# Two more chunk pairs per feed-forward stage by seven products, the weight pools taken in another order, and the bias broadcasts cut in eight

## The chip, the core and the metric

The kernel runs on one core of one Trainium2 chip. A core has five engines that work side by side, each through its own list of instructions in order: TensorE (PE) multiplies matrices into PSUM, VectorE (DVE) and ScalarE (ACT) do elementwise work, GpSimd (POOL) does small elementwise work and issues some transfers, SyncE (SP) issues most transfers. They wait for each other by semaphores. The metric is the device time of one execution, in microseconds (us); the time of a kernel is the median of its runs.

## What is computed

Two layers, each of three stages on a sequence of 512 tokens with 1024 features, all in 32-bit floats. Every stage ends in a residual sum and a layer norm.

```python
D_MODEL, SEQ, DEPTH, D_FF = 1024, 512, 2, 2816

def _swiglu(x, w1, w2):
    gt, up = jnp.split(x @ w1, 2, axis=-1)
    return (jax.nn.silu(gt) * up) @ w2

for l in range(DEPTH):
    x = _layer_norm(DN_ALPHA * x + 0.5 * _swiglu(x, ffn1_w1[l], ffn1_w2[l]), ln1_g[l], ln1_b[l])
    mix = _token_mix(x, w_in[l], ..., rel_bias, w_br_a[l], w_br_b[l], w_br_c[l], w_gate[l], b_gate[l], w_out[l])
    x = _layer_norm(DN_ALPHA * x + mix, ln2_g[l], ln2_b[l])
    x = _layer_norm(DN_ALPHA * x + 0.5 * _swiglu(x, ffn2_w1[l], ffn2_w2[l]), ln3_g[l], ln3_b[l])
```

`_swiglu` is the feed-forward stage (FFN). It occurs four times, twice in each layer, and is what the change touches. `_token_mix` holds three kinds of attention; one of them adds a bias that depends on the distance of two tokens and is made from `rel_bias`.

## The kernel before

**Precision by three products.** A matrix product in 32-bit precision is made of three products in a faster format: each operand is split into a rounded part and the rest (`hi` and `lo` for weights, `xh` and `xl` for the activations), and hi·xh + hi·xl + lo·xh is summed in PSUM. A weight chunk therefore goes through three steps: a transfer into one of three `raw` buffers (L153), a rounding copy into `hi` on ScalarE (L146), and `lo = raw - hi` on VectorE (L147).

**The first half of an FFN.** `w1` has 2 x 2816 columns, in chunks of 128. A *pair* f (0 to 21) is the chunk of the gate and the chunk of the up part that belong together; it makes one tile `ha` or `hb` of the hidden layer, 128 features by 512 tokens. Pairs 0 and 1 are done by `staged`, in token halves, while the transposes of the last tokens still arrive. Pairs 2 to 21 run in the loop of `ffn` (L392 on), in one of two ways:

- A *plain* pair (f in `PLAIN`, L275): two projections, each 8 chunks of features x 3 products with 512 columns, so 48 matmuls (L167 to L169). Then `evac` (L332) computes silu times up: one step on ScalarE (L334), two on VectorE (L335, L336).
- A *seven-product* pair (`strassen`, L349, its weights from `seven`, L280): the pair is written as a product of 2x2 blocks (gate and up by the two halves of the features; tokens in two halves), and seven block products replace eight. Each is 4 x 3 matmuls with 256 columns, so 84 matmuls in all (L357). They need sums of weights (`ws`, L293 to L296), split like weights (L298, L299) into the units `u1` and `u2`; half of the up chunk split alone (`dh`, `dl`, L300, L301); and four sums of tokens, split into `th` and `tl`. The token sums are made once in each FFN, by `token_sums` (L305 to L320), in VectorE's order behind pair 2's call. The products come in a fixed order: the gate's unit `ug`, `u1` with the first token sum, `u1` with the second, `u2` with the third, `ud` with the fourth, then `ug` and `u2` with the tokens themselves. VectorE then puts the results together (L368 to L376).

**Where split weights lie.** A *unit* is one `hi` and one `lo` tile. `unit` (L130) hands them out in turn from a list `seq` of pools, position `more.n % len(seq)`: three from `wt`, two from `more.pool` where that is open (it is, in every FFN), two from `nx.w1` while the loop of pairs runs. `nx.w1` is the pool `w1p`, which is opened when the pairs begin and lies where `xa` was, the tokens in their untransposed form (and, in the first FFN, where the tables of `init` were). Its tiles can be written only when those have been read: `xa` is first sent to `x_sp` in HBM by four transfers from POOL's queue (L381). `th`, `tl`, `dh`, `dl`, `ws`, `sn` and `v` lie in `w1p` too. The counter `more.n` runs on from one stage to the next, so an FFN begins its pairs at whatever place of the list the counter has reached: in the first FFN that is the first of the two `w1p` units.

**The start of the kernel.** The first FFN also runs `tables` between the pairs of `staged` and pair 2: on TensorE some small products (L1281, L1287) and transposes (L1292, L1294), on VectorE the tables `ctab`, `vm`, `peT`, `bgate`. Two rows of bias values go to `bsml` in HBM (L1299), and from there two transfers spread them to `bvec`, 8 heads x 128 rows x 384 values each, 1.57 MB (L395). The attention of the first mix stage reads `bvec` from 381.9 us of the span on (L496).

**The second half of an FFN** (`rows_ln`) multiplies the hidden layer with `w2`, 22 row chunks, 24 matmuls of 512 columns each (L180 to L182), and ends in the layer norm. Two hidden tiles are split early, into a unit of `wt`, when pair 21 is reached.

**Order.** TensorE's and POOL's instructions run in the order of the program text. Those of VectorE, ScalarE and SyncE are ordered when the kernel is built, by a planner that estimates when each becomes ready. Each engine then keeps its order: an instruction that waits holds back all behind it.

Of the kernel before, what the change touches and what calls it, by code (L numbers as in the profile page):

```python
# [9 lines left out]
F32 = mybir.dt.float32  # L10
# [8 lines left out]
P = 128  # L19
S, D, F = 512, 1024, 2816  # L20
KD, KF, NB = D // P, F // P, S // P
H, DH, NSLOT = 8, 64, 32
# [4 lines left out]
TLEN = 3 * P  # L27
# [37 lines left out]
def body(tc, a, out, depth=DEPTH):  # L65
    nc = tc.nc
    PE, POOL = mybir.EngineType.PE, mybir.EngineType.Pool

    def pool(name, bufs=1, side=None, **kw):
        return tc.alloc_tile_pool(name=name, bufs=bufs, side=side, **kw)  # L70

    const = pool("const")
    xtp = pool("xtp")
    wt = pool("wt")
# [6 lines left out]
    def ps(tag=None, name="ps", shape=(P, 512)):  # L81
        if tag is None:
            tag = PS_ALL[ring[0] % 8]
            ring[0] += 1
        return psp.tile(list(shape), F32, name=name, tag=tag, bufs=PS_TAGS[tag])
# [16 lines left out]
    bgate = const.tile([P, depth, 3, KD], F32, name="bgate")  # L102
    peT = const.tile([P, depth, 2, 32], F32, name="peT")
    stats = [const.tile([P, 8], F32, name=f"st{i}") for i in range(NB)]
    const.tile([P, 48], F32, name="pad")

    xh = xtp.tile([P, KD, S], F32R, name="xh")
    xl = xtp.tile([P, KD, S], F32R, name="xl")
# [1 line left out]
    bsml = dram.tile([2, H, TLEN], F32, name="bsml")  # L110
    bvec = dram.tile([2, H, P, TLEN], F32, name="bvec")
# [6 lines left out]
    more = K()  # L118
# [9 lines left out]
    nx = K()  # L128
    nx.pool = nx.w1 = None

    def unit():

        if nx.pool:
            pl, nb = nx.pool, 4
        else:
            seq = [(wt, 3)] * 3 + [(more.pool, 2)] * 2 * bool(more.pool) + [(nx.w1, 2)] * 2 * bool(nx.w1)
            more.n += 1
            pl, nb = seq[more.n % len(seq)]
        return [pl.tile([P, KD, P], F32R, name=n, tag=n, bufs=nb) for n in ("hi", "lo")]
# [123 lines left out]
    def staged(wts, pend):  # L263

        pts = [ps(name="pj") for _ in wts]
        for i, (o, w) in enumerate(zip(pts, wts)):
            proj(o, w, halves[0])
            if i in pend:
                pend[i]()
        for o, w in zip(pts, wts):  # L270
            proj(o, w, halves[1])
        return pts

    NTAIL = 4
    PLAIN = (0, 1, 2, 3, 4, 5, 14)  # L275

    def ffn_first(w1):
        return [wcols(w1, c) for c in (0, F, P, F + P)]
# [1 line left out]
    def seven(w1, f):  # L280

        v = w1.rearrange("(k p) f -> p k f", p=P)
        rg, ru = wraw(), wraw()
        nc.sync.dma_start(rg, v[:, :, f * P:(f + 1) * P])
        nc.sync.dma_start(ru, v[:, :, F + f * P:F + (f + 1) * P])
        ug, u1, u2 = wsplit(rg), unit(), unit()
        ud = [nx.w1.tile([P, 4, P], F32R, name=n, tag=n) for n in ("dh", "dl")]
        h1, h2 = slice(0, 4), slice(4, 8)  # L290
        x1, x2 = [nx.w1.tile([P, KD, P], F32, name="ws", tag="ws", bufs=2) for _ in range(2)]
        tt = nc.vector.tensor_tensor
        tt(x1[:, h1], ru[:, h1], ru[:, h2], op=OP.add)  # L293
        tt(x1[:, h2], x1[:, h1], rg[:, h1], op=OP.subtract)  # L294
        tt(x2[:, h1], rg[:, h1], ru[:, h1], op=OP.subtract)
        tt(x2[:, h2], rg[:, h2], x1[:, h2], op=OP.subtract)  # L296
        for (hi, lo), x in ((u1, x1), (u2, x2)):
            nc.scalar.activation(hi, x, AF.Copy)  # L298
            tt(lo, x, hi.bitcast(F32), op=OP.subtract)  # L299
        nc.scalar.activation(ud[0], ru[:, h2], AF.Copy)  # L300
        tt(ud[1], ru[:, h2], ud[0].bitcast(F32), op=OP.subtract)  # L301
        return ug, u1, u2, ud
# [20 lines left out]
    def ffn(l, w1, w2, which, xap, xa, wts, pend, done_prev, last, nxt):  # L323


        st = K()
        NA = KF - NTAIL

        def hpart(f):
            return (st.ha, st.hb)[f >= NA][:, f - NA * (f >= NA)]  # L330

        def evac(f, pg, pu):  # L332
            t = st.lnp.tile([P, S], F32, name="t", tag="t", bufs=3)
            nc.scalar.activation(t, pg, AF.Tanh, scale=0.5)  # L334
            nc.vector.scalar_tensor_tensor(t, t, 1.0, pg, op0=OP.add, op1=OP.mult)  # L335
            nc.vector.tensor_tensor(hpart(f), t, pu, op=OP.mult)  # L336

        hs = {}

        def h_parts(k, t):  # L340
            nc.scalar.activation(t[:, 0], hpart(k), AF.Copy)
            nc.vector.tensor_tensor(t[:, 1], hpart(k), t[:, 0].bitcast(F32), op=OP.subtract)
            hs[k] = t

        H1, H2 = slice(0, 256), slice(256, 512)

        def strassen(f, ws):
            (ug, u1, u2, ud), (t1, t2, t3, t4) = ws, st.t
            ga, pa, pb = ps(name="pg"), ps(name="pu"), ps(name="pv")  # L349
            p_, r_, s_ = [(xh[:, k:k + 4, c], xl[:, k:k + 4, c]) for k, c in ((0, H1), (4, H1), (4, H2))]  # L350

            def prod(o, w, k0, x, first=True):
                for k in range(4):
                    hi, lo = w[0][:, k0 + k], w[1][:, k0 + k]
                    vh, vl = x[0][:, k], x[1][:, k]
                    for i, (wx, vx) in enumerate(((hi, vh), (hi, vl), (lo, vh))):
                        nc.tensor.matmul(o, wx, vx, start=first and k == 0 and i == 0, stop=k == 3 and i == 2,  # L357
                                         skip_group_check=True)

            tt = nc.vector.tensor_tensor  # L360
            prod(ga[:, H1], ug, 0, p_)
            prod(ga[:, H2], u1, 0, t1, False)
            sn = st.w1p.tile([P, S], F32, name="sn", tag="sn", bufs=2)
            nc.scalar.activation(sn, ga, AF.Copy)
            prod(pa[:, H1], u1, 4, t2)
            prod(pa[:, H2], u2, 0, t3, False)
            v = st.w1p.tile([P, S], F32, name="v", tag="v", bufs=2)
            tt(v[:, H1], pa[:, H1], sn[:, H1], op=OP.add)  # L368
            tt(v[:, H2], pa[:, H2], v[:, H1], op=OP.add)
            prod(pb[:, H1], ud, 0, t4)  # L370
            u = hpart(f)
            tt(u[:, H1], pb[:, H1], v[:, H2], op=OP.add)
            tt(u[:, H2], sn[:, H2], v[:, H2], op=OP.add)
            prod(ga[:, H1], ug, 4, r_, False)
            prod(ga[:, H2], u2, 4, s_, False)
            tt(ga[:, H2], ga[:, H2], v[:, H1], op=OP.add)  # L376
            evac(f, ga, u)

        pts = staged(wts, pend)
        for tb in range(NB):  # L380
            nc.gpsimd.dma_start(x_sp[tb * P:(tb + 1) * P, :], xa[tb])  # L381
        done_prev()
        xap.release()
        fb = pool("fb", reuse_waits="tile")
        st.lnp = pool("lnp", reuse_waits="tile")
        fa = pool("fa", reuse_waits="tile")
        st.hb = fb.tile([P, NTAIL, S], F32, name="hb")
        st.ha = fa.tile([P, NA, S], F32, name="ha")
        st.w1p = nx.w1 = pool("w1p", side="right", reuse_waits="tile")
        evac(0, pts[0], pts[1])  # L390
        evac(1, pts[2], pts[3])
        for f in range(2, KF):  # L392
            if after and f in (10, 14):
                i = after.pop()
                nc.gpsimd.dma_start(bvec[i], bsml[i, :, None, :].to_broadcast([H, P, TLEN]))  # L395
            if f == KF - 1:
                for k, n in enumerate(("hi", "lo")):
                    h_parts(k, wt.tile([P, KD, P], F32R, name=n, tag=n, bufs=3)
                            .rearrange("p (a b) c -> p a (b c)", a=2))
            if f not in PLAIN:  # L400
                strassen(f, seven(w1, f))
                continue
            wg, wu = wcols(w1, f * P), wcols(w1, F + f * P)
            pg, pu = ps(name="pg"), ps(name="pu")
            proj(pg, wg)
            proj(pu, wu)
            evac(f, pg, pu)
            if f == 2:
                token_sums(st)
        nx.w1 = None  # L410
        st.w1p.tile([P, 88], F32, name="pad")
        st.w1p.release()
        xap, xa = alloc_xa()
        for tb in range(NB):
            nc.gpsimd.dma_start(xa[tb], x_sp[tb * P:(tb + 1) * P, :])
        hsp = pool("hsp", side="right", reuse_waits="tile")
        ln = LN(hsp, which, l, xa, 0.25, last)

        def wload(k):
            if k not in hs:  # L420
                h_parts(k, hsp.tile([P, 2, S], F32R, name="hs", tag="hs", bufs=6))
            return wrows(w2, k)

        wts, pend = rows_ln(KF, wload, lambda k: hs[k][:, 0], lambda k: hs[k][:, 1], ln, NA, fa.release, nxt)

        def done():
            nx_close()
            hsp.release()
            st.lnp.release()
            fb.release()  # L430

        return wts, pend, done, xap, xa
# [812 lines left out]
            pre.append(wcols(first_w, 0, 2))  # L1245
            pre.append(wcols(first_w, F, 2))

    after = [0, 1]
    init = pool("init", side="right")

    def tables_load():
# [110 lines left out]
```

## Time and profile before

| | us |
|---|---|
| median of 3 runs | 2520.06 (2519.49 to 2521.06) |
| profiled execution, its own time | 2518.52 |
| its span on the core | 2516.8 |
| TensorE busy in the span | 2484.7 |
| VectorE busy | 1617.8 |
| ScalarE busy | 1077.9 |
| GpSimd busy | 213.1 |

The profile is of one execution. A row of a timeline has the start in us from the span's start, the time in us, the engine, the line, the operation, output<-inputs, the shape and a count of merged instructions; in brackets stand the engine's idle time before it and what ended that. A matmul's time there is longer than the distance to the next, since matmuls overlap in the array; what a matmul costs is the distance between two starts. The row of a group has a count, the busy time and the mean of one in ns, then the idle time before them. In the rows of slices each digit is the busy share of a fortieth of the span, in tenths; PEclk is TensorE's granted clock in tenths of full speed.

### The profile page before, as it was taken

How to read it: one execution, taken by the hardware profiler on the slowest of the kernel's cores; microseconds unless marked ns; L12 is line 12 of the kernel's file. 1: busy time of each engine (PE TensorE's matmuls, PEld its weight loads, DVE VectorE, ACT ScalarE, POOL GpSimd, SP SyncE). 2: the span in 40 equal slices, each digit the busy share in tenths (PEclk: the TensorE clock that was granted, in tenths of full speed). 3: DMA queues.
4: the chain of work that ended last, by engine and by line, in shares of the span. 5: the costliest groups of instructions: out<-in, count | busy, mean ns of one | idle time of the engine just before them, and what ended most of it. 6: DMA issues, size and time to landing. Idle time of an engine off the chain costs nothing.

```text
span 2516.8 us, 39571 instructions
## 1 busy us (share of the span) xinstructions
PE 2484.7 (99%) x15259; PEld 2173.9 (86%) x15259; DVE 1617.8 (64%) x3309; ACT 1077.9 (43%) x2107; POOL 213.1 (8%) x424
## 2 busy tenths in 40 slices
PE   7999999999999999999999999999999999999998
PEld 7999888788888888998889998877888888899987
DVE  5788455577753468884477883556776534788834
ACT  3344333476642233443343442345766322344432
POOL 2000000133300000000000000001332000000000
PEclk8999999999999999999999999999999999999999
DMA  7333434633143342334332353435321434323431
GB/s 235 91 105 110 152 102 124 180 86 85 47 138 97 122 126 83 111 109 151 117 109 76 105 163 102 140 109 155 89 77 43 146 101 139 109 77 109 140 127 59
DMA packets 378476, 286.11 MB, mean 114 GB/s; under 512 B 17928, under 2 KB 349848, under 8 KB 378288
## 3 DMA queue, kind: packets, MB, share of 16 engines
q1 hardware_dynamic: 370496, 258.68, 35.1%
q0 software_dynamic: 7792, 24.91, 2.7%
q8 instruction: 120, 1.97, 0.3%
q14 instruction: 68, 0.56, 0.1%
HBM read 256.22 MB, written 17.88 MB: 109 GB/s over the span
## 4 chain that ended last, share of the span: by engine, by line
PE 47%; DVE 1%; DMA 1%; ACT 1%; issue 0%; POOL 0%; DVEq 0%; POOLq 0%; ACTq 0%; SPq 0%
PE pg L357 7%; PE pu L357 3%; PE acc L181 3%; PE acc L180 3%; PE acc L182 3%; PE pj L167 3%; PE pj L168 3%; PE pj L169 3%; PE pv L357 2%; PE gate L167 1%; PE gate L168 1%; PE gate L169 1%; PE brp L169 1%; PE brp L168 1%; PE brp L167 1%; PE sN L881 1%
## 5 line engine op out<-in xcount | busy, mean ns | idle before, releaser
L147 DVE TENSOR_TENSOR lo<-raw,hi 128x1024 fp32r<-128x1024 f32 (+2 forms) x354 | 416.0, 1182 | 524.9 <-ACT hi L146 514.4
L146 ACT ACTIVATE hi<-raw 128x1024 fp32r<-128x1024 f32 (+2 forms) x354 | 359.8, 1025 | 717.9 <-PE acc L181 225.4
L167 PE MATMUL pj<-xh,hi 128*128 128x512 f32 (+1 forms) x720 | 266.7, 370 | 0.1
L168 PE MATMUL pj<-xl,hi 128*128 128x512 f32 (+1 forms) x720 | 254.7, 354 | 2.3 <-DVE xl L227 2.3
L169 PE MATMUL pj<-xh,lo 128*128 128x512 f32 (+1 forms) x720 | 254.5, 353 | 0.0
L180 PE MATMUL acc<-hi,hs 128*128 128x512 f32 x640 | 249.5, 390 | 0.0
L182 PE MATMUL acc<-lo,hs 128*128 128x512 f32 x640 | 249.1, 389 | 0.0
L181 PE MATMUL acc<-hi,hs 128*128 128x512 f32 x640 | 249.0, 389 | 0.0
L357 PE MATMUL pg<-xh,lo 128*128 128x256 f32 x720 | 203.8, 283 | 0.0
L357 PE MATMUL pg<-xl,hi 128*128 128x256 f32 x720 | 203.8, 283 | 0.0
L357 PE MATMUL pg<-xh,hi 128*128 128x256 f32 x720 | 203.7, 283 | 0.0
L298 ACT ACTIVATE hi<-ws 128x1024 fp32r<-128x1024 f32 x120 | 126.0, 1059 | 161.1 <-DVE ws L294 52.2
L299 DVE TENSOR_TENSOR lo<-ws,hi 128x1024 fp32r<-128x1024 f32 x120 | 145.8, 1219 | 36.1 <-ACT hi L298 36.0
L169 PEld LDWEIGHTS pj<-xh,lo 128*128 128x128 f32 x720 | 136.1, 189 | 19.7
L167 PEld LDWEIGHTS pj<-xh,hi 128*128 128x128 f32 x720 | 136.5, 190 | 15.3 <-issue 3.1
L168 PEld LDWEIGHTS pj<-xl,hi 128*128 128x128 f32 x720 | 136.7, 190 | 14.8 <-DVE xl L227 3.2
L181 PEld LDWEIGHTS acc<-hi,hs 128*128 128x128 f32 x640 | 120.2, 188 | 24.9
L182 PEld LDWEIGHTS acc<-lo,hs 128*128 128x128 f32 x640 | 120.1, 188 | 24.9
L180 PEld LDWEIGHTS acc<-hi,hs 128*128 128x128 f32 x640 | 120.2, 188 | 24.6
L357 PEld LDWEIGHTS pg<-xl,hi 128*128 128x128 f32 x720 | 138.2, 192 | 0.3
L357 PEld LDWEIGHTS pg<-xh,hi 128*128 128x128 f32 x720 | 138.2, 192 | 0.3
L357 PEld LDWEIGHTS pg<-xh,lo 128*128 128x128 f32 x720 | 138.2, 192 | 0.0
(323 smaller groups left out, 6016.5 us busy)
## 6 DMA issues: line engine op xcount, KB each, us to landing
raw<-in_ffn_w_dram SPq DMA_DIRECT2D x264, 512.0 KB, 3.8
raw<-in_w_in_dram SPq DMA_DIRECT2D x56, 512.0 KB, 4.0
raw<-in_w_gate_dram SPq DMA_DIRECT2D x48, 512.0 KB, 3.9
x_sp<-xa POOLq DMA_DIRECT2D x24, 512.0 KB, 5.1
ks<-hl SPq DMA_DIRECT2D x96, 128.0 KB, 2.4
xa<-x_sp POOLq DMA_DIRECT2D x16, 512.0 KB, 4.5
raw<-in_w_out_dram SPq DMA_DIRECT2D x16, 512.0 KB, 3.4
tab<-bvec SPq DMA_DIRECT2D x16, 256.0 KB, 4.1
```

Of the source, the lines that this page charges most:

```text
L146: nc.scalar.activation(hi[:, c], raw[:, c], AF.Copy)
L147: nc.vector.tensor_tensor(lo[:, c], raw[:, c], hi[:, c].bitcast(F32), op=OP.subtract)
L167: nc.tensor.matmul(o, hi[:, k], vh, start=first, stop=False)
L168: nc.tensor.matmul(o, hi[:, k], vl, start=False, stop=False)
L169: nc.tensor.matmul(o, lo[:, k], vh, start=False, stop=last)
L180: nc.tensor.matmul(o, sh(k)[:, t], hi[:, c], start=k == 0, stop=False)
L181: nc.tensor.matmul(o, sl(k)[:, t], hi[:, c], start=False, stop=False)
L182: nc.tensor.matmul(o, sh(k)[:, t], lo[:, c], start=False, stop=k == nk - 1)
L298: nc.scalar.activation(hi, x, AF.Copy)
L299: tt(lo, x, hi.bitcast(F32), op=OP.subtract)
L357: nc.tensor.matmul(o, wx, vx, start=first and k == 0 and i == 0, stop=k == 3 and i == 2, skip_group_check=True)
L881: nc.tensor.matmul(o[:, 0:nb].rearrange("p k b j -> p (k b j)"), q, kx[:, 2 * b0:2 * (b0 + nb)].rearrange("p a b -> p (a b)"), start=i == ...
```

## The change

Three edits, in four places of the text, and a tile that gets a name:

- `PLAIN` shrinks from seven pairs to five: pairs 4, 5 and 14 go over to seven products, pair 12 becomes plain. Of the 22 pairs, 17 go by seven products instead of 15, in each of the four FFNs. The first seven-product pair is now pair 4 instead of pair 6, and the runs between plain pairs are 8 and 9 long instead of 8 and 7.
- `unit` takes the pools, while `w1p` is open, in the order `wt`, `more`, `more`, `w1p`, `w1p`, `wt`, `wt`, and the counter is set to 4 when `w1p` opens, so that every FFN begins at the sixth place: three units of `wt`, two of `more`, two of `w1p`, and round again. The number of units is the same.
- The broadcasts to `bvec` are issued in eight transfers of two heads each, at pairs 6 to 13 instead of two transfers at pairs 10 and 14; ahead of each, POOL copies one column of the hidden tile of three pairs before into `pace`, a column of a tile that was there as padding, and so waits until that tile exists.

```diff
@@
-    const.tile([P, 48], F32, name="pad")
+    pace = const.tile([P, 48], F32, name="pace")[:, 0:1]
@@ def unit():
         if nx.pool:
             pl, nb = nx.pool, 4
         else:
-            seq = [(wt, 3)] * 3 + [(more.pool, 2)] * 2 * bool(more.pool) + [(nx.w1, 2)] * 2 * bool(nx.w1)
+            seq = [(wt, 3)] * 3 + [(more.pool, 2)] * 2 * bool(more.pool)
+            if nx.w1:
+                seq = seq[2:] + [(nx.w1, 2)] * 2 + seq[:2]
             more.n += 1
             pl, nb = seq[more.n % len(seq)]
@@
-    PLAIN = (0, 1, 2, 3, 4, 5, 14)
+    PLAIN = (0, 1, 2, 3, 12)
@@ def ffn(...):
         st.w1p = nx.w1 = pool("w1p", side="right", reuse_waits="tile")
+        more.n = 4
         evac(0, pts[0], pts[1])
         evac(1, pts[2], pts[3])
         for f in range(2, KF):
-            if after and f in (10, 14):
-                i = after.pop()
-                nc.gpsimd.dma_start(bvec[i], bsml[i, :, None, :].to_broadcast([H, P, TLEN]))
+            if after and f >= 6:
+                i, h = after.pop(0)
+                nc.gpsimd.tensor_copy(pace, hpart(f - 3)[:, 0:1])
+                nc.gpsimd.dma_start(bvec[i, h:h + 2], bsml[i, h:h + 2, None, :].to_broadcast([2, P, TLEN]))
@@
-    after = [0, 1]
+    after = [(i, h) for i in range(2) for h in range(0, H, 2)]
```

## The prediction

> **What bounds the kernel now.** I read the page's first lines, then TensorE's timeline where pairs begin, then the places where it waits.
>
> ```profile
> span 2516.8 us, 39571 instructions
> PE 2484.7 (99%) x15259; PEld 2173.9 (86%) x15259; DVE 1617.8 (64%) x3309; ACT 1077.9 (43%) x2107; POOL 213.1 (8%) x424
> ...
> PEclk8999999999999999999999999999999999999999
> ```
>
> TensorE is busy 99% of the span, and its clock is full but for the first fortieth. So the time can fall in two ways: fewer or shorter matmuls, or the removal of one of its few waits. The starts of pairs show what a pair costs.
>
> ```profile
> 60.94 0.39 PE L167 MATMUL pg<-xh,hi 128*128 128x512 f32 x1
> ...
> 71.82 0.39 PE L167 MATMUL pg<-xh,hi 128*128 128x512 f32 x1
> ...
> 103.65 0.28 PE L357 MATMUL pg<-xh,hi 128*128 128x256 f32 x1
> ...
> 113.73 0.28 PE L357 MATMUL pg<-xh,hi 128*128 128x256 f32 x1
> ```
>
> These are the starts of the plain pairs 3 and 4 and of the seven-product pairs 7 and 8 of the first FFN. A plain pair takes 71.82 - 60.94 = 10.88 us (48 matmuls, 0.2267 each), a seven-product pair 113.73 - 103.65 = 10.08 (84 matmuls, 0.120 each).
>
> The large wait is ahead of pair 2 of the first FFN:
>
> ```profile
> 34.17 3.21 PE L1281 MATMUL ct<-init,init 128*128 128x32 f32 x28
> ...
> 38.79 0.30 PE L1294 MATMUL peT<-ident,init 64*128 64x64 f32 x2
> 46.66 0.79 PE L167 MATMUL pg<-xh,hi 128*128 128x512 f32 x1 [7.58 <-ACT hi L146]
> ...
> 49.13 0.63 PE L168 MATMUL pg<-xl,hi 128*128 128x512 f32 x1
> 49.56 0.63 PE L169 MATMUL pg<-xh,lo 128*128 128x512 f32 x1
> ```
>
> TensorE stands still for 7.58 us until ScalarE has rounded pair 2's weights. After that two matmuls lie 0.43 apart instead of 0.227: the clock has halved. Pair 2 takes 60.94 - 46.66 = 14.28 us, 3.40 more than its neighbour.
>
> **Part 1: two more pairs by seven products.** In each FFN three plain pairs of 10.88 become seven-product pairs and one goes the other way: 2 x 0.80 = 1.60 us, over four FFNs 6.40. This stands only if VectorE keeps up, since a seven-product pair gives it much more to do.
>
> ```profile
> 1044.20:1064.30 20.10, 20.10 (x170) 20.10 (x169) 17.35 (x27) 10.73 (x14) 0.00 (x0) 1.00 0.55 157
> 1064.30:1075.20 10.90, 10.90 (x50) 9.05 (x49) 10.87 (x18) 3.21 (x4) 0.00 (x0) 1.00 0.33 98
> ```
> ```profile
> 1045.06 1.22 DVE L299 TENSOR_TENSOR lo<-ws,hi 128x1024 fp32r<-128x1024 f32 x1
> ```
> ```profile
> 1054.25 0.28 PE L357 MATMUL pg<-xh,hi 128*128 128x256 f32 x1
> ```
>
> The first two rows are windows of the second FFN (columns: length, then busy time of PE, weight loads, DVE, ACT, POOL, then clock, DMA share, GB/s). VectorE has 17.35 us in two seven-product pairs, 8.7 of 10.08 each. Pair 13, last of a run of eight, starts at 1054.25; its `u1`, used 1.44 us into it (one product of 12 x 0.120 down), was split by 1046.28: 9.4 us ahead. Since VectorE's 8.7 is below 10.08, a run of nine keeps most of that lead; if it lost a whole 1 us with the ninth, nothing would wait.
>
> The tight place is new: the first seven-product pair is pair 4, only two plain pairs (21.8 us) behind the start of pair 2, and VectorE must have made the token sums by then. Rows of the second FFN before:
>
> ```profile
> 940.15 0.40 PE L167 MATMUL pg<-xh,hi 128*128 128x512 f32 x1
> ```
> ```profile
> 940.95 4.62 DVE L314 TENSOR_TENSOR ha<-xh,xl 128x1024 f32<-128x1024 f32 x4
> 945.50 2.35 DVE L147 TENSOR_TENSOR lo<-raw,hi 128x1024 fp32r<-128x1024 f32 x2
> 947.76 1.22 DVE L317 TENSOR_TENSOR hb<-ha 128x1024 f32<-128x1024 f32 x1
> ...
> 952.90 1.22 DVE L320 TENSOR_TENSOR tl<-hb,th 128x1024 fp32r<-128x1024 f32 x1
> 954.04 0.68 DVE L293 TENSOR_TENSOR ws<-raw 128x512 f32<-128x512 f32 x1
> 954.64 0.68 DVE L295 TENSOR_TENSOR ws<-raw 128x512 f32<-128x512 f32 x1
> ```
>
> Pair 2 starts at 940.15; VectorE's token sums cannot start before 940.95, since their place in `ha` held the weights of `staged`. From there on, by the distance between starts (1.14 for 1024 columns, 0.60 for 512), the changed build lists this ahead of the last split token sum: the four sums 4.55; four differences and four splits 8 x 1.14 = 9.1; four weight sums and one of pair 5, 5 x 0.60 = 3.0; `dl` 0.60; splits of `u1`, `u2` and of pair 5's `ug` 3 x 1.14 = 3.4; three evacuation steps 1.8. In all 22.5: done at 963.4. The product that needs it is the fifth, 48 x 0.12 = 5.76 into pair 4, which starts at 940.15 + 21.8 = 961.9: at 967.7. That leaves 4.3 us; `u2`, done at 961.7 and needed at 966.3, has 4.6. The splits of pairs 2 and 3 and of pair 4's `ug` stand ahead of 940 in the build, so they are not in the sum. I take a wait of 0 here; the bounds are 0 and 4 us in each of three FFNs (a slip of twice the margin).
>
> The Trainium skill's page "TensorE: Matmul & The Clock Gate" (section "Wait — 56ns, not 53.3ns?") puts a warm matmul at N / 2.4 GHz plus 2.5 ns, so 215.8 ns for 512 and 109.2 for 256 columns; as an estimate by it a swap would save 48 x 0.2158 - 84 x 0.1092 = 1.19 us and part 1 would be 9.5. The starts above give 0.227 and 0.120, and the measurement decides.
>
> **Part 2: the pools turned.** Why pair 2 waits:
>
> ```profile
> 24.44 1.07 POOL L381 DMA_DIRECT2D x_sp<-xa  x2 [0.22 <-issue]
> 25.54 0.22 POOL L1297 TENSOR_SCALAR sinks<-sinks 128x16 f32<-128x16 f32 x1
> 39.07 0.57 POOL L1299 DMA_DIRECT2D bsml<-init  x1 [13.31 <-DVE init L1288]
> 41.50 0.52 POOL L1299 DMA_DIRECT2D bsml<-init  x1 [1.86 <-DVE init L1288]
> 44.98 2.22 POOL L395 DMA_DIRECT2D bvec<-bsml  x2 [2.96 <-DMA bsml<-init]
> ```
> ```profile
> 38.44 1.06 ACT L146 ACTIVATE hi<-raw 128x1024 fp32r<-128x1024 f32 x1 [4.71 <-DVE ctab L1283]
> 44.61 2.95 ACT L146 ACTIVATE hi<-raw 128x1024 fp32r<-128x1024 f32 x3 [5.12 <-DMA raw<-in_ffn_w_dram]
> ```
>
> Pair 2 gets the two `w1p` units, which lie over `xa` and `init`. `init` is read last by the second transfer to `bsml`, issued at 41.50 and landed just before 44.98, where POOL stops waiting for it. ScalarE's order has these two roundings as the second and third of the group at 44.61, behind a weight that landed then; two of three raw buffers hold pair 2's weights all that time, so the others go through one.
>
> After the change pair 2 takes two units of `wt`, one unused, one free when TensorE leaves the first weight of `staged`. That is three weights ahead of the end of `staged`, of 24 x 0.120 = 2.9 us each, which is where `ct` begins: 34.17 - 3 x 2.9 = 25.5. With 1.06 on ScalarE and 1.22 on VectorE it is ready by 28, and pair 2 can start when the transposes end, 38.79 + 0.30 = 39.09. Gain: 46.66 - 39.09 = 7.57, and 3.40 for the clock, which then stays full.
>
> What is late next? Pair 3 has `wt` and `more`, free at 28.4 and 31.3 by the same count. Pair 4 (due at 39.09 + 21.8 = 60.9) has `more`, then both `w1p` units, and `dh`, `th`, `tl` lie over `xa` and `init` too; all are open when `bsml` has landed, by 45. VectorE then has four splits of token sums, weight sums, `dl`, three splits and an evacuation, about 12 us: ready near 54, 8 us before `u1` is due. So the cover is there; without it this gain would turn into a wait at pair 4.
>
> The Trainium skill (same page, "Part 1: The HAM clock gate") has the clock halve after an idle window of about 3.4 us and return after about 3.4 us of work; by that, as an estimate, the restart would cost half of 3.4, 1.7 us, not the 3.40 of the row, and the sum be 16.5. The trace stayed slow for longer, and it decides.
>
> In the other three FFNs pair 2 waits for nothing (pair 3 follows 10.9 us behind), so the turn gains nothing there. The last pair of the first FFN gains:
>
> ```profile
> 245.59 0.28 PE L357 MATMUL pg<-xh,hi 128*128 128x256 f32 x1
> ...
> 248.05 0.38 PE L357 MATMUL pg<-th,lo 128*128 128x256 f32 x1 [0.61 <-DVE lo L299]
> ...
> 256.54 0.40 PE L180 MATMUL acc<-hi 128*128 128x512 f32 x1
> ```
>
> Pair 21 takes 10.95, 0.87 too long: its units were all of `wt` and `more`, with one `wt` unit lent to the hidden tiles, so one waited for pair 20. With the count begun anew it gets two `w1p` units and a `wt` unit last used by pair 19, as in the three FFNs that have no such wait. Gain 0.87.
>
> **Part 3: the broadcasts.** The same bytes in eight pieces. POOL has no other work from 47.2 us on for the 189.3 of its next wait, so the copies, 0.22 each by its smallest row above, hold up nothing.
>
> ```profile
> POOL xa L415 <- PE pg L357: 189.3, 1, 189.3
> ```
> ```profile
> raw<-in_ffn_w_dram SPq DMA_DIRECT2D x264, 512.0 KB, 3.8
> ...
> bvec<-bsml POOLq DMA_DIRECT2D x2, 1536.0 KB, 13.9
> ```
>
> A quarter of a broadcast's 13.9 us, 3.5, bounds from above what a piece can add to a weight transfer's 3.8; below, 0. It meets a pair every 10 us whose split weights are some 9 us ahead, and the next transfers wait for TensorE's release anyway, so delays don't add up: 0. Without that lead it would be up to 8 x 3.5 = 28 us. The burst that now ties up the transfers from 45 to 61 us is gone, which only adds cover.
>
> **Part 4: the rest.** Outside the FFNs the build gives every engine the same order as before; `pace` is the former padding. Nothing.
>
> **The sum.** 6.40 + 7.57 + 3.40 + 0.87 = 18.24 us. The span of 2516.8 becomes 2498.6, the profiled execution's 2518.52 becomes 2500.3. The median of the runs, 2520.06, lies 1.54 above that execution, so I expect 2520.06 - 18.24 = 2501.8, and with a rest for small waits at the new changes between kinds of pairs 2502.
>
> **Rivals.**
>
> *A, short waits at pair 4 of the later FFNs.* For: 22.5 us of VectorE's work in 26.8, in fixed order between ScalarE's steps. Against: 4.3 us of margin, counted at measured distances. Up to 4 us in each of three FFNs: 2503 to 2514.
>
> *B, the start still waits.* If the wait at 46.66 were due to the weights' arrival and not to where they are put, the 10.97 us stay: 2520.06 - 6.40 - 0.87 = 2512.8. For: ScalarE's row at 44.61 names a transfer. Against: the group's first weight waited for that, and TensorE was let go by a rounding whose place was the pool over `x`.
>
> *C, slower: the token sums become the bound.* In the three later FFNs the last token sum would come so late that TensorE stands still as long as it now does at the start, and its clock halves: 3 x (7.57 + 3.40) = 32.9 lost against 18.2 gained, 2534.7. It decides from a wait of 6.1 us in each (18.2 / 3), so from sums 10.4 us later than I count. For: VectorE has worked 85% of this stretch before (37.16 of 43.50 us):
>
> ```profile
> 940.20:983.70 43.50, 43.50 (x194) 35.99 (x194) 37.16 (x42) 14.08 (x16) 0.00 (x0) 1.00 0.25 73
> ```
>
> Against: with pairs 4 and 5 still plain, that stretch also held the preparation of pairs 6 to 8; what pair 4 needs is the first 22.5 us of it.
>
> *D, no gain per pair.* If VectorE's waits for ScalarE and transfers made a seven-product pair in a run of nine as long as a plain one, and B held too, the time would stay: 2519. Against: every seven-product pair of the profile but the last of the first FFN takes 10.08.
>
> **How the numbers follow.** My forecast has 0.70, A 0.12, B 0.08, C 0.06, D 0.04. The likeliest time is 2502. Its own range reaches down to 2499.5 (the runs before spread 1.6 us, and a wait I don't count may go) and, with most of A, up to 2511; B, C and D are left out, 0.18. A measurement of this kernel tells a change from none at 0.2%, 5.0 us. Faster by more: the forecast, A and B, 0.90; within: D, 0.04; slower: C, 0.06.
>
> **What would show it.** In the changed profile pair 2 of the first FFN should start near 39.1 with no idle time before it and take 10.9; pair 4 should start near 60.9, and in the second FFN 21.8 after pair 2, with no idle time named at `pg` or `pu`; the second digit of the clock's row should be full; 68 x 84 = 5712 matmuls at the seven products; the span 2498.6. Idle time at pair 4 behind a DVE `tl` or `lo` means A or C, at pair 2 behind an ACT `hi` means B, and seven-product pairs longer than 10.1 mean D. The prediction is wrong if the span is above 2508.

## The result and the profile after

The changed kernel takes 2530.56 us, median of 6 runs (2527.75 to 2532.51), against 2519.76 for the kernel before (6 runs beside it): a ratio of 1.0043 (95% interval 1.003 to 1.0056). It is slower by 10.8 us where 17.8 of gain from this median were forecast. Its profiled execution took 2531.19. The first lines of its page, busy time by engine and the clock's row:

```profile
span 2529.3 us, 40222 instructions
...
PE 2489.0 (98%) x15547; PEld 2191.5 (87%) x15547; DVE 1656.1 (65%) x3397; ACT 1089.2 (43%) x2131; POOL 224.8 (9%) x438
...
PEclk9989999999999999999999999999999999999999
```

TensorE has 15547 - 15259 = 288 more matmuls, eight pairs of 84 instead of 48: the change does what it says. The loss is in a few pairs of the first FFN. The view of windows, one row for each of pairs 6 to 12 (bounds and length, then busy time of PE, weight loads, DVE, ACT and POOL with their counts, then clock, DMA share, GB/s):

```profile
84.32:94.40 10.08, 10.08 (x86) 10.08 (x85) 5.14 (x8) 2.85 (x4) 0.55 (x1) 1.00 0.47 139
94.40:112.17 17.77, 13.16 (x86) 12.55 (x85) 9.47 (x15) 4.55 (x6) 1.57 (x2) 0.82 0.29 84
112.17:127.56 15.39, 12.31 (x85) 11.70 (x85) 10.26 (x16) 5.07 (x7) 1.57 (x2) 0.88 0.32 93
127.56:150.82 23.26, 12.36 (x86) 11.95 (x85) 13.37 (x23) 6.03 (x8) 2.59 (x4) 0.78 0.22 66
150.82:160.90 10.08, 10.08 (x87) 10.08 (x85) 6.16 (x9) 2.62 (x4) 1.45 (x3) 1.00 0.65 173
160.90:176.93 16.03, 12.89 (x87) 12.49 (x85) 9.52 (x16) 6.58 (x9) 0.96 (x2) 0.80 0.37 111
176.93:188.06 11.13, 11.13 (x50) 9.20 (x49) 10.45 (x17) 3.83 (x5) 1.15 (x2) 0.98 0.48 141
```

Pairs 7, 8, 9 and 11 take 7.69, 5.31, 13.18 and 5.95 us more than the 10.08 of pair 6, and pair 12 takes 0.22 more than the 10.91 of its fellows in the other FFNs: 32.35 us. TensorE is not busy in 21.7 us of this; the rest is its clock, whose mean is 0.78 to 0.88 in these four rows. What it waits for, from the view of waits between 60 and 190 us (engine, tile and line, what it waited for, us in total, times, longest):

```profile
ACT hi L148 <- DMA raw<-in_ffn_w_dram: 34.4, 9, 9.0
...
DVE ws L295 <- DMA raw<-in_ffn_w_dram: 19.8, 5, 6.1
...
PE pg L359 <- ACT sn L366: 16.8, 4, 10.7
...
PE pv L359 <- DVE dl L303: 4.1, 4, 1.4
...
PE pv L359 <- ACT dh L302: 0.8, 2, 0.5
```

TensorE never waits for the `hi` or `lo` of a unit here. It waits for `sn`, a copy of its own result that ScalarE takes out of PSUM, and, 4.9 us, for `dl` and `dh`, the half of the up chunk that is split alone. But ScalarE waits for weights, 34.4 us, and so does VectorE with its weight sums, 19.8 us. The timeline of pair 9 shows how one becomes the other (a row of each engine's own timeline: POOL, SP, ACT, PE):

```profile
131.51 0.51 POOL L398 COPY pace<-ha 128x1 f32<-128x1 f32 x1 [13.57 <-DVE ha L338]
132.10 1.05 POOL L399 DMA_DIRECT2D bvec<-bsml  x1
...
132.98 0.37 SPq L288 DMA_DIRECT2D raw<-in_ffn_w_dram  x1
...
144.00 1.06 ACT L148 ACTIVATE hi<-raw 128x1024 fp32r<-128x1024 f32 x1 [9.04 <-DMA raw<-in_ffn_w_dram]
144.96 0.58 ACT L336 ACTIVATE t<-pg 128x512 f32<-128x512 f32 x1
145.44 0.59 ACT L366 ACTIVATE sn<-pg 128x512 f32<-128x512 f32 x1
...
146.08 0.58 PE L359 MATMUL pg<-xh,hi 128*128 128x256 f32 x1 [10.73 <-ACT sn L366]
```

The pacing copy ends when a hidden tile is there. POOL then issues a piece of the broadcast at 132.10, and 0.88 us later SyncE issues the next weight, whose raw buffer came free in the same stretch. That weight lands only just before 144.00, 11 us later. Its rounding belongs to a later pair, but in ScalarE's list it stands ahead of `t` and `sn` of the current one. `sn` comes at 145.44, and TensorE, whose next products go into the tile that `sn` reads, goes on at 146.08 after 10.73 us.

In pairs 7 and 8 the late weight stops VectorE first: its weight sums start at 96.58 and 113.13, after 6.1 and 6.0 us of waiting. What VectorE does next frees a raw buffer and makes the hidden tile for which the pacing copy waits, so the next piece and the next weight are issued in the same instant, at 100.34 and again at 116.89. The copies wait for a tile of three pairs before, so what the program places at pairs 6 to 13 is issued during pairs 4 to 12, at 65.75, 83.78, 100.34, 116.89, 132.10, 149.98, 159.85 and 177.19 us.

The median landing of the two kinds of transfers, in the list of DMA issues (KB each, us from issue to landing):

```profile
raw<-in_ffn_w_dram SPq DMA_DIRECT2D x264, 512.0 KB, 3.9
...
bvec<-bsml POOLq DMA_DIRECT2D x8, 384.0 KB, 11.4
```

A piece with a quarter of the bytes takes 11.4 us, where a whole broadcast took 13.9.

### The profile page after: what moved, and what is told of

It is laid out like the page before. It is cut to its first block, busy times and chain, and to the rows that moved or that the text cites. A ratio compares the mean times of both kernels' runs of the same rounds, so it can differ in the third digit from the quotient of the medians.

```text
span 2529.3 us, 40222 instructions
## 1 busy us (share of the span) xinstructions
PE 2489.0 (98%) x15547; PEld 2191.5 (87%) x15547; DVE 1656.1 (65%) x3397; ACT 1089.2 (43%) x2131; POOL 224.8 (9%) x438
## 4 chain that ended last, share of the span: by engine, by line
PE 94%; DMA 3%; DVE 2%; ACT 1%; issue 1%; DVEq 0%; POOLq 0%; ACTq 0%; SPq 0%; POOL 0%
PE pg L359 14%; PE acc L182 7%; PE acc L183 7%; PE acc L184 7%; PE pu L359 7%; PE pj L169 5%; PE pj L170 5%; PE pj L171 5%; PE pv L359 3%; PE gate L169 3%; PE gate L170 3%; PE gate L171 3%; DMA raw<-in_ffn_w_dram 3%; PE brp L169 2%; PE brp L170 2%; PE brp L171 2%
## 5 line engine op out<-in xcount | busy, mean ns | idle before, releaser
L359 PE MATMUL pg<-xh,hi 128*128 128x256 f32 x816 | 235.2, 288 | 16.8 <-ACT sn L366 16.8
L359 PE MATMUL pg<-xl,hi 128*128 128x256 f32 x816 | 234.4, 287 | 0.0
L359 PE MATMUL pg<-xh,lo 128*128 128x256 f32 x816 | 234.3, 287 | 0.0
L359 PEld LDWEIGHTS pg<-xh,hi 128*128 128x128 f32 x816 | 160.4, 197 | 17.9 <-ACT sn L366 17.6
L301 DVE TENSOR_TENSOR lo<-ws,hi 128x1024 fp32r<-128x1024 f32 x136 | 165.2, 1219 | 4.5 <-ACT hi L300 4.4
L359 PEld LDWEIGHTS pg<-xl,hi 128*128 128x128 f32 x816 | 160.5, 197 | 0.3
L359 PEld LDWEIGHTS pg<-xh,lo 128*128 128x128 f32 x816 | 160.3, 196 | 0.0
L359 PE MATMUL pu<-th,hi 128*128 128x256 f32 x544 | 154.0, 283 | 0.0
L359 PE MATMUL pu<-tl,hi 128*128 128x256 f32 x544 | 154.0, 283 | 0.0
L359 PE MATMUL pu<-th,lo 128*128 128x256 f32 x544 | 153.9, 283 | 0.0
L170 PEld LDWEIGHTS pj<-xl,hi 128*128 128x128 f32 x720 | 137.1, 190 | 11.4
```

The source lines that it names most:

```text
L170: nc.tensor.matmul(o, hi[:, k], vl, start=False, stop=False)
```

## The experiments

The three theories that the first expectations name: N, the pieces are narrow (two heads outermost) and so take long and hold up the weights that are issued with them; B, the bytes sent while seven-product pairs run, in whatever form; V, VectorE's work or the pools, so not the broadcasts at all. Each ratio below is against the kernel before, run on the same chip.

**e1: the whole broadcasts back.** The changed kernel with the two transfers of the kernel before and without pacing copies.

```diff
-            if after and f >= 6:
-                i, h = after.pop(0)
-                nc.gpsimd.tensor_copy(pace, hpart(f - 3)[:, 0:1])
-                nc.gpsimd.dma_start(bvec[i, h:h + 2], ...)
+            if after and f in (10, 14):
+                i = after.pop()
+                nc.gpsimd.dma_start(bvec[i], bsml[i, :, None, :].to_broadcast([H, P, TLEN]))
```

> The changed kernel with the two whole broadcasts of before (pairs 10 and 14, no pacing copies) in place of the eight pieces. Theory N (narrow pieces: each piece keeps two of the sixteen DMA engines busy for some 11 us, and a weight transfer, which needs all sixteen, ends behind it): no idle time at pg, pu or pv in pairs 4 to 12 of the first FFN, time near 2500 us (2519.8 less 6.4, 7.7, 0.9 and about 5). Theory V (VectorE or the pools hold up the seven-product pairs of the first FFN): the waits of 20 us and more in pairs 7 to 11 stay, 2525 to 2535.

Measured: 2497.64 us, ratio 0.9923 (0.9908 to 0.9938). Every seven-product pair takes 10.08. V falls: the whole loss belongs to the broadcasts and their copies.

**e2: pieces with the rows outermost.** The same eight pieces at the same places, 128 rows outermost instead of two heads.

```diff
-                nc.gpsimd.dma_start(bvec[i, h:h + 2], bsml[i, h:h + 2, None, :].to_broadcast([2, P, TLEN]))
+                nc.gpsimd.dma_start(bvec[i, h:h + 2].rearrange("h p t -> p h t"),
+                                    bsml[i, None, h:h + 2, :].to_broadcast([P, 2, TLEN]))
```

> The changed kernel with the same eight pieces at the same places with the same copies, but with the 128 rows as the outermost dimension of each transfer and the two heads inside. Theory N: a piece runs on all engines and lands in 2 to 5 us instead of 11, the waits in pairs 7 to 11 go, time 2499 to 2504. Theory B (the bytes of a paced broadcast hold up the weights, however they are laid out): pieces still near 11 us, time 2525 to 2535.

Measured: 2503.14 us, ratio 0.9945 (0.993 to 0.996). The same bytes land in less than half the time, and of TensorE's 16.8 us of waits for `sn` 4.4 are left. Its list of DMA issues, then its waits from 38 to 190 us:

```profile
bvec<-bsml POOLq DMA_DIRECT2D x8, 384.0 KB, 5.0
```
```profile
PE pg L359 <- ACT sn L366: 4.4, 3, 2.2
```

So the form of the transfer carries most of the loss, as N has it. Three pairs of the profiled execution still lose 6.7 us in all (5.5 from e1 by the medians): in this form too, pieces issued one by one are not free. Whether the rest is due to their bytes or to the copies wasn't tested.

**e3: the pieces alone.** The kernel before with only the broadcasts of the changed one.

> The kernel before with only the eight paced pieces. Theory N: waits in the first FFN's pairs 7 to 13 of the same kind, 20 to 35 us in all, time 2540 to 2555. Theory V: nothing, 2520.

Measured: 2549.63 us, ratio 1.0129 (1.0114 to 1.0144), with pairs 9, 10, 11 and 13 at 22.75, 18.46, 17.39 and 14.81 us. The pieces cost 32.3 us without any of the rest.

**e6: whole broadcasts, paced.** The changed kernel with one whole broadcast at pair 6 and one at pair 10, behind the pacing copies.

> The changed kernel with two whole broadcasts, each behind a pacing copy, at pairs 6 and 10. A whole broadcast has eight heads, so by theory N it lies on eight engines with the same bytes on each as a piece has on its two, and holds up the weights for as long as one piece, but twice instead of eight times: a quarter of the 32 us, time 2503 to 2513. Theory B (by bytes): the same bytes, the same waits, 2525 to 2535.

Measured: 2507.08 us, ratio 0.9957 (0.9941 to 0.9974). The first costs nothing, the second 9.3 us (pairs 9 and 10).

**e8: four pieces of four heads**, paced, at pairs 6 to 9.

```diff
-                nc.gpsimd.dma_start(bvec[i, h:h + 2], bsml[i, h:h + 2, None, :].to_broadcast([2, P, TLEN]))
+                nc.gpsimd.dma_start(bvec[i, h:h + 4], bsml[i, h:h + 4, None, :].to_broadcast([4, P, TLEN]))
-    after = [(i, h) for i in range(2) for h in range(0, H, 2)]
+    after = [(i, h) for i in range(2) for h in range(0, H, 4)]
```

> The changed kernel with four broadcasts of four heads, 768 KB each, at pairs 6 to 9, instead of eight of two heads. If a transfer's landing goes by the two-to-eight outermost heads (each piece lands in 10 to 13.5 us whatever its size), half as many pieces cost about half of the 33 us that eight cost beside two whole ones behind no copies: 2509 to 2519, waits in pairs 7 to 10 only. If the cost goes by the bytes sent while pairs run, it stays at 2526 to 2532.

Measured: 2520.63 us, ratio 1.0011 (1.0001 to 1.002), some 22 us above e1 (each against the kernel before on its own chip) and between the two expectations. Pairs 7 and 8 take 23.94 and 17.69, all others their normal time. The landings fit N, but the cost doesn't go by the number of pieces: eight cost 32 us, four cost 21.5. In both kernels no pair waits until two pieces have landed and the third is issued or about to be (pair 7); until then the lead of the weights takes up the delay: in the changed kernel a weight issued at 66.82, 1.07 us behind the first piece, takes 10.84 us, and TensorE waits for nothing. These are rows of windows in which, after the weights' other shares have landed, little but a broadcast is left in flight: three rows of the changed kernel, of which the first is still ahead of that, then one of e8 and one of e6 (the second number from the right is the DMA share):

```profile
137.00:139.00 2.00, 0.00 (x0) 0.00 (x0) 0.12 (x1) 0.00 (x0) 0.00 (x0) 1.00 0.96 297
139.00:141.00 2.00, 0.00 (x0) 0.00 (x0) 0.00 (x0) 0.00 (x0) 0.00 (x0) 0.72 0.14 55
141.00:143.00 2.00, 0.00 (x0) 0.00 (x0) 0.00 (x0) 0.00 (x0) 0.00 (x0) 0.50 0.13 41
```
```profile
91.00:93.00 2.00, 2.00 (x19) 2.00 (x18) 0.00 (x0) 0.00 (x0) 0.00 (x0) 1.00 0.26 102
```
```profile
127.00:129.00 2.00, 2.00 (x19) 2.00 (x18) 0.00 (x0) 0.00 (x0) 0.00 (x0) 1.00 0.49 174
```

Of 16 DMA engines, 0.13 is two, 0.26 four, 0.49 eight: as many as there are heads in the outermost dimension. Worked out from this, each engine gets 192 KB whatever the piece (384 / 2, 768 / 4, 1536 / 8), and the landings are alike: 11.4, 11.7 and 13.4 us. With the rows outermost it took 5.0. The Trainium skill's page "DMA: Bandwidth & Descriptors" (section "Rules for kernel authors") states this: an outermost dimension smaller than 16 confines the whole transfer to at most so many engines, and a multiple of 16 belongs there. The shares agree.

The trace's DMA packets show what then happens to the two weights issued at 132.98 and 133.87, 1024 KB in all. By 139 us their queue has moved 905 KB. From 139 to 142 us it moves only 43 packets of 512 bytes, 21.5 KB, while the piece moves 30 packets of 4608 bytes, 135 KB. The last 97 KB of the weights, 194 such packets, pass from 142.4 us on, when the piece is all but through. By these numbers the late part of a weight is its portion on the engines of the piece: there the two get through by about as many packets each, but a weight's packets are a ninth in size. A weight issued in the same instant as a piece comes through ahead of it: those of 100.34 and 116.89 land in 4.4 and 4.3 us, those issued 0.9 to 2.4 us behind a piece (66.82, 102.71, 132.98, 133.87) in 10.4 to 11.6.

**e9: the same pieces at once.** The changed kernel without the pacing copies. POOL then issues the eight pieces from 40.97 us on, when the first bias row has landed.

```diff
-                nc.gpsimd.tensor_copy(pace, hpart(f - 3)[:, 0:1])
```

> The changed kernel without the pacing copies: the same eight pieces, each two heads outermost, but POOL issues all of them as soon as the bias rows are in HBM (some 45 us), during plain pairs 2 to 4, where the whole broadcasts went. If a piece costs because it is narrow and comes when a weight is due soon, eight at once in that place should share the engines, be done by 60 to 75 us and cost few waits: 2497 to 2505. If eight narrow pieces cost as much wherever they stand, 2520 to 2532.

Measured: 2497.86 us, ratio 0.992 (0.9903 to 0.9936): one line taken out turns 10.8 us above the kernel before into 20.1 below. Its windows, first the stretch in which all pieces are in flight, then pairs 7 and 11:

```profile
41.00:66.10 25.10, 25.10 (x124) 21.31 (x124) 16.22 (x19) 8.23 (x10) 8.52 (x8) 0.98 0.77 191
...
92.58:102.66 10.08, 10.08 (x87) 10.08 (x85) 9.35 (x16) 3.27 (x6) 0.00 (x0) 1.00 0.35 104
...
132.90:143.60 10.70, 10.33 (x87) 10.12 (x85) 8.90 (x16) 5.17 (x7) 0.00 (x0) 1.00 0.51 149
```

Narrow pieces cost next to nothing when they all run together in this place: TensorE is busy all through this stretch, and later only pair 11 loses 0.62. They share the engines (0.77 of them busy), delay the weights of this stretch once instead of in each pair, and stand in plain pairs, which have no `sn` or `dh`. Which of these matters most isn't shown, since no run sends narrow pieces at once among seven-product pairs. But neither the width alone (e9) nor the pace alone (e2) makes most of the loss: it is narrow transfers issued one by one among the weights of seven-product pairs.

**e4: the pools alone**, **e5: the pairs alone.** The kernel before with the order of the pools and `more.n = 4` alone, and with the shorter `PLAIN` alone.

> Before, with the order of the pools and the count begun at 4 alone: no new seven-product pairs, broadcasts as before. From the changed kernel's trace: pair 2 of the first FFN near 39 to 40.5 without idle time, taking 12.6 to 12.8 us, so pair 3 some 7.6 us earlier than before; the last pair of the first FFN 10.08 (0.87 gained); the short waits at the starts of later stages gone (up to 4 us). Sum 8.5 to 12.5 us: 2505 to 2510. By the prediction's working it would be 11.84 us (7.57 + 3.40 + 0.87), with pair 2 taking 10.9. If instead the whole broadcasts, which now run beside other weights, cost waits, the time stays above 2512.

> Before, with the two more seven-product pairs alone. By the pairs' lengths (10.88 and 10.08) 4 x 1.60 = 6.4 us are gained: 2511 to 2513, pair 2 still waits 7.6 us. If the earlier first seven-product pair needed the turned pools (token sums or the units over x late at pair 4), idle time at pair 4 would take some of it back: 2514 to 2520.

Measured: e4 2508.09 us, ratio 0.9958 (0.9943 to 0.9973), as expected; e5 2516.3, ratio 0.999 (0.9981 to 0.9999): the time lies in the second range expected, but TensorE doesn't wait at pair 4, which was to be its reason. Alone they give 9.9 and 1.7 us, together (e1) 19.7. In e5 every FFN has its 1.60 us, but the unit count runs on, so in FFNs 2 and 4 pair 21 takes 12.44 and pair 5 10.98, and in the third pair 2 takes 12.36, where 10.08, 10.08 and 10.91 are normal: 2 x 2.36 + 2 x 0.90 + 1.45 = 8.0 us back, more than the 6.4. What e5 still gains comes from the start, where pair 3 begins 4.61 us earlier than before (at 56.33 us). Pair 21 of its second FFN waits for the rounding and the rest of a weight sum, as pair 21 of the first does for a rest in the kernel before:

```profile
1133.16 0.39 PE L357 MATMUL pu<-th,hi 128*128 128x256 f32 x1 [1.09 <-ACT hi L298]
1134.42 0.39 PE L357 MATMUL pu<-th,lo 128*128 128x256 f32 x1 [0.76 <-DVE lo L299]
```

e1 is e4 and e5 together and has none of these waits, so the turned pools and the count begun anew are what lets the shorter `PLAIN` keep its gain. Which unit is late at pair 21 I didn't trace. e5 also says something of the start, where pair 2 comes at 40.97 with the pools not turned. Rows of ACT, PE and POOL:

```profile
38.91 2.95 ACT L146 ACTIVATE hi<-raw 128x1024 fp32r<-128x1024 f32 x3 [4.73 <-DMA raw<-in_ffn_w_dram]
...
40.97 0.80 PE L167 MATMUL pg<-xh,hi 128*128 128x512 f32 x1 [1.89 <-ACT hi L146]
...
41.97 0.52 POOL L1299 DMA_DIRECT2D bsml<-init  x1 [2.52 <-DVE init L1288]
43.95 2.21 POOL L395 DMA_DIRECT2D bvec<-bsml  x2 [1.46 <-DMA bsml<-init]
```

Pair 2's two roundings, again behind another weight in a group of three, are done by 41.86, before the transfer that reads the second bias row out of `init` is even issued (41.97). So that row is not what holds them back. In the kernel before, ScalarE's list has one more weight ahead of them, by the order of the transfers pair 4's second, and it landed at 44.61; in e5 pair 4 goes by seven products, and there this weight isn't rounded by itself.

**e7: the tables' small products spread.** e1 with the 14 small products `ct` interleaved with the second halves' products of pairs 0 and 1, one each, instead of in one run ahead of pair 2.

```diff
-            proj(o, w, halves[1])
+            for k in range(KD):
+                proj(o, w, halves[1], range(k, k + 1))
+                if mid:
+                    mid.popleft()()
...
 def tables(...):
-        for j in range(14):
...
```

> The changed kernel with the two whole broadcasts of before (2497.64 when run), and the 14 small products of the tables interleaved, one each, between the second half's products of the first two pairs, instead of in one run ahead of pair 2. If the run of small products is what lowers TensorE's clock at pair 2 (no idle time is left there), fewer of them in a row let pair 2 take 10.9 to 11.6 instead of 12.6: 2494.5 to 2496.5. If the clock falls whatever stands there (the transposes alone, or something of the first 40 us), pair 2 keeps 12.6 and the time is 2497 to 2499.

Pair 2 now takes 11.02 us, from 39.10 to 50.12. The windows of e1, then those of e7:

```profile
30.00:40.00 10.00, 10.00 (x73) 8.53 (x72) 9.25 (x14) 6.39 (x7) 1.09 (x2) 0.96 0.55 162
40.00:50.00 10.00, 10.00 (x41) 8.12 (x40) 10.00 (x11) 4.08 (x5) 2.21 (x2) 0.87 0.56 191
```
```profile
30.00:40.00 10.00, 10.00 (x75) 8.55 (x74) 8.28 (x11) 4.87 (x6) 0.57 (x1) 1.00 0.57 163
40.00:50.00 10.00, 10.00 (x46) 8.26 (x45) 10.00 (x15) 6.31 (x8) 2.73 (x3) 1.00 0.43 141
```

TensorE is busy all the time in both, and only the run of small products is gone: it was this run that halved the clock. By narrower windows e1's clock is 1.00 up to 39.1 us, 0.50 from 39.2 to 42.5, and 1.00 again after 42.7. Pair 2 comes out as the first expectation has it, but the time doesn't follow: 2497.11 us, ratio 0.9914 (0.9899 to 0.9929), not distinguishable from e1. Of the 1.21 us that pair 3 starts earlier, 0.83 goes in a wait at pair 11, and the rest in the mix stage, where I didn't follow it.

**e10: e7 with whole broadcasts, rows outermost.**

> The changed kernel with two whole broadcasts unpaced, written with 128 rows outermost instead of eight heads, and with the tables' small products spread between other products as before. If landing goes by the outermost size, 1536 KB should land in under 10 us instead of 14.7, and pair 11's wait of 0.8 us goes: 2495 to 2497. If landing goes by the bytes, 13 to 15 us and 2497 to 2498.

Measured: 2497.64 us, ratio 0.9919 (0.9904 to 0.9934), landings 11.3 us: neither faster nor as short as expected. With both broadcasts in flight at once, 3 MB over 16 engines is, as an estimate, 192 KB each again, whichever way they are cut. Pairs 9 to 11 lose 1.8 us.

e1, e7, e9 and e10 all beat both kernels, by some 20 us against the kernel before, and can't be told apart.

## Why the prediction was wrong

The terms, in us gained; the right column is worked out from the starts of pairs and stages in the two profiles:

| step | forecast | measured |
|---|---|---|
| Part 1, eight pairs by seven products | 6.40 | 6.40 |
| Part 2, start of pair 2 of the first FFN | 7.57 | 6.16 |
| Part 2, clock in pair 2 | 3.40 | 1.49 |
| Part 2, pair 21 of the first FFN | 0.87 | 0.87 |
| Part 3, broadcasts in pieces | 0 | -32.35 |
| starts of later stages and the end | not counted | 4.94 |
| sum (spans 2516.8 and 2529.3) | 18.24 | -12.49 |

**Part 3 is the step that failed**, twice. Its bound, "A quarter of a broadcast's 13.9 us, 3.5", took a transfer's time to go by its bytes. By the landings it goes by the bytes on each engine: a quarter of the heads is also a quarter of the engines, and a piece takes 11.4. And the cover, "It meets a pair every 10 us whose split weights are some 9 us ahead", looked at TensorE's need of the weights alone. A late weight stops ScalarE, whose list holds `sn`, `dh` and `t` of the current pair behind it, and VectorE, whose weight sums wait for it, and what stands behind these has no such lead. "The next transfers wait for TensorE's release anyway" was wrong too: in the view of SyncE's waits of the kernel before (60 to 190 us) they wait mostly for VectorE's `ws`, `lo` and `dl` and never for TensorE, so a late weight makes the next one late. Nor did "delays don't add up" hold: nothing waits at first, but from pair 7 on four of five pairs do. The worst case named there, 28 us "without that lead", is near what came only by chance: it counts 3.5 for each of eight pieces, and what came are 5.3 to 13.2 us in four pairs. "The burst that now ties up the transfers from 45 to 61 us is gone, which only adds cover" had it the wrong way round: in e1 and e9 that burst costs next to nothing, where it is, in plain pairs.

**Part 2.** The wait at pair 2 went as forecast, but my cause for it was wrong: in e5, with the pools not turned, pair 2 starts 5.69 us earlier than before, while `init` is still being read. Rival B's reading, a transfer ahead of pair 2's roundings in ScalarE's list, was nearer to it; its consequence, that the turn of the pools would not help, is refuted by e4. The clock's 3.40 was put down to the 7.58 us of idle time. But in the kernel before the clock stands at half from 39.4 us on, 0.3 us after that wait begins. And the changed kernel has no idle time there (rows of `tables` and the start of pair 2):

```profile
37.40 2.67 PE L1291 MATMUL bv<-init 32*8 32x384 f32 x4
...
40.14 0.44 PE L1298 MATMUL peT<-ident,init 64*128 64x64 f32 x2
40.50 0.79 PE L169 MATMUL pg<-xh,hi 128*128 128x512 f32 x1
...
41.52 0.63 PE L171 MATMUL pg<-xh,lo 128*128 128x512 f32 x1
41.95 0.63 PE L169 MATMUL pg<-xh,hi 128*128 128x512 f32 x1
```

Matmuls are again 0.43 apart, and `bv` already takes 2.67 us. The clock falls during the run of small products or just behind it (at 37.5 us here), as e7 shows, which also makes pair 2 start 1.4 later than the 39.09 counted at full clock.

**Part 1 and the rivals.** The pairs took what was counted, in the later FFNs as well (starts of pairs 2, 3 and 4 of the second):

```profile
961.01 0.40 PE L169 MATMUL pg<-xh,hi 128*128 128x512 f32 x1
...
971.92 0.39 PE L169 MATMUL pg<-xh,hi 128*128 128x512 f32 x1
...
982.80 0.28 PE L359 MATMUL pg<-xh,hi 128*128 128x256 f32 x1
```
```profile
L359 PE MATMUL pu<-th,hi 128*128 128x256 f32 x544 | 154.0, 283 | 0.0
```

Pair 4 follows 21.79 us behind pair 2, and no product waits for a token sum in any FFN; seven-product pairs that no late weight delays take 10.08: A, C and D are refuted. What I didn't see is that this part would have been worth nothing without Part 2: in e5 its 6.4 us are lost again in the pairs. Where the units lie decides that, not VectorE's load, at which I had looked.

**Not foreseen.** Waits at the starts of later stages, which the kernel before had, are gone (view of waits of the kernel before):

```profile
PE pj L168 <- DVE xl L227: 2.3, 3, 0.9
PE hid L653 <- DMA cw<-in_cmp_k_w_dram: 1.7, 2, 1.3
```

They make up most of the 4.94; why they go I didn't follow, and e4 still has 1.9 us at `hid`. The last 1.10 of it, at the end of the kernel, isn't there in e1, and I didn't follow it. Without Part 3 the changes are worth 20 us, a little more than the sum forecast. That the two agree is in part luck: in e1 pair 2 takes 12.61, so the clock's term comes to 1.67 of the 3.40, and waits that weren't counted make up for it.

## What to carry to other kernels

Before a transfer is cut in pieces, look at what its outermost dimension becomes, since that sets how many engines it runs on: here a quarter of the bytes took four fifths of the time. And ask of a transfer that is made late not only when its data is needed, but which instruction waits for it and what stands behind that one in its engine's list. Pacing a burst over many steps can turn one delay in a slack stretch into one in each step of a tight one.

## What the runs showed of the hardware

- A transfer spread over few DMA engines delays wide ones of another queue that are issued shortly behind it: weights that otherwise land in 3.9 us took 10.4 to 11.6 when issued 0.9 to 2.4 us behind a piece on two engines, although the other 14 engines were then nearly idle (a share of 0.13). Issued in the same instant as a piece, they took 4.4 and 4.3.
- On these two engines the queues got about as many packets each, not as many bytes: 43 packets of 512 bytes for the weights and 30 of 4608 for the piece from 139 to 142 us.
- TensorE's clock fell to half without idle time, during or just behind a run of small products (granted clock 0.50 from 39.2 to 42.5 us in e1), and stayed full when large products stood between them (1.00 from 30 to 50 us, e7).
